# A hybrid decoder layer on one core: the first norm's root one step earlier, and four first loads issued from ACT's queue

## The chip, the cores and the metric

The kernel runs on one core of one Trainium2 chip. The core has a matrix engine (PE, TensorE), a vector engine (DVE), a scalar engine (ACT), GpSimd (POOL) and a sync engine (SP), each with its own in-order queue of instructions, and 16 DMA engines that all queues share. DMA transfers are issued by an instruction on SP, ACT or POOL; most of the weights are issued on SP. The metric is the device time of one execution, in microseconds (us). Before the change it was 1701.68 us, the median of 3 runs (1701.42 to 1701.92).

## The reference

One decoder layer is run on 256 prompt rows and on 8 groups of 8 sample rows, together 320 rows of width 2048. All is float32. Cut to what matters:

```python
def rms_norm(x, g):
    xf = x.astype(jnp.float32)
    y = xf * lax.rsqrt(jnp.mean(xf * xf, axis=-1, keepdims=True) + EPS)
    return (y * g.astype(jnp.float32)).astype(x.dtype)

def decoder_layer(x, ...):
    xn = rms_norm(x, g_mix)
    z = xn @ w_in            # parts B, C, h, q, k, v, gate_conv, gate_attn
    u = c_gate * h_conv
    conv_out, conv_state = short_conv(u, conv_prev, w_conv)
    y_conv = (b_gate * conv_out) @ w_conv_out
    attn = ...               # banded window of 128, 16 query heads, 4 kv heads, sinks
    y_attn = attn @ w_attn_out
    merged = sigmoid(gate_c) * y_conv + sigmoid(gate_a) * y_attn
    h = x + merged @ w_o
    hn = rms_norm(h, g_ffn)
    h = h + (silu(hn @ w_gate) * (hn @ w_up)) @ w_down
    return h, conv_state, k_state, v_state
```

The output is a last RMSNorm of h, with the updated key, value and convolution states. What the change touches is the first line, `rms_norm(x, g_mix)`, and the product with the k and v columns of `w_in` that follows it.

## The kernel before

**Layout.** Rows are tokens in the reference; the kernel keeps activations transposed, with 128 of the 2048 features on the partitions and the 320 tokens along the free axis. A block is such a piece of 128 features; there are 16, numbered 0 to 15.

**Two halves for each operand.** Every product is made of three float32r products: each operand is split into a high part (an ACT copy that rounds, `whi` or `xh_t`) and a low part (a DVE subtraction, `wlo` or `xl_t`), and PE accumulates hi x hi, lo x hi and hi x lo. Weights pass through a raw tile `wraw` (4 buffers), filled by a DMA on SP; `split_to` (L92 to L94) makes `whi` on ACT (L93) and `wlo` on DVE (L94), 3 buffers each. A transfer into a raw buffer waits until the split of the tile that was there is done.

**The start.** `x_load(i)` (L223) fetches columns of x: x is cut into five column blocks of 2, 2, 4, 4 and 4 feature blocks (`XB`), and each is three transfers, two of 128 prompt rows and one of 64 sample rows. In block 0 the second prompt transfer is on ACT's queue; all others are on SP's. `g_mix` is loaded on ACT's queue into `vrow` (L231). Nine products on a constant tile (`wm`, L235) come first on PE; then `g_mix` is turned by a PE transpose (`pv`, L237) and copied by DVE (L238).

**The norm.** The gain `g_mix` is applied to x while it is transposed: `x_prep(kc)` (L242) makes three PE transposes of block kc into `pt`, an ACT copy with the scale g_mix to `xh_t` (L247), the DVE remainder `xl_t` (L248), and a DVE copy of the plain x to `hT` (L253). The root of the mean square, one number for each token, is applied only after the product. The squares are summed on ACT (`squares`, L323), 512 columns at a time. `rstd_of` (L175) then scales the sum (L178), and `inv_root` takes Sqrt on ACT (L185, with a load of its function table), a reciprocal on DVE (L186) and one Newton step on DVE (L187, L188, L190). The result `r3` has a token on each partition; three diagonal matrices `dg` (L367, DVE) and three products with ones (`prb`, L368, PE) spread it over all partitions, and DVE copies it to `rb` (L376).

**The first product.** `kv_product` (L268) multiplies x by the 512 k and v columns, with four accumulators, in nine weight tiles of 1, 1 and then seven times 2 feature blocks. `x_prep(kc + 2)` is issued ahead of the last accumulator of block kc, so that x is prepared while PE multiplies. In the last tile (blocks 14 and 15) the order goes by accumulators, and the fourth accumulator's products are placed behind prb. After the product DVE multiplies the accumulators by `rb` (`kT` L378, `vT` L380), which frees them; the next product, q, takes the same accumulators and waits for that.

**The side work.** `start_rest` (L327) is a generator that holds the small work of the start in steps. `tick` runs it to its next `yield`, once behind each weight tile but the last, and once within the last tile, ahead of accumulator 2 of block 14. Step by step, it issues small loads, squares of columns 0 to 511, nothing, squares of columns 512 to 1023, of 1024 to 1535, of 1536 to 2047 with the sum `s3` (L350) and the copy of `st_sb` (L356), nothing, and in the ninth step, within the last tile, the root and prb. A scheduler orders the instructions of each engine from this program order, from dependencies and from hints given by `after(...)`, so a step that moves in the program need not move by as much on every engine.

**What follows.** Behind the first product comes q (four pairs of columns, `load_q`), beside it the k and v rows are written out, and two transfers of 960 KB from DRAM to DRAM (`cache_shift`, L427) shift the caches. They stand on SP's queue behind the last weight transfers of q's first pair and ahead of those of the second. Then come C, H, B, the gates, the two output products, w_o, and the feed-forward products, all bound to the same two-half scheme.

Of the kernel before, what the change touches and what calls it, by code (L numbers as in the profile page):

```python
# [26 lines left out]
P = 128  # L27
# [13 lines left out]
def hybrid_layer(ctx: ExitStack, tc: tile.TileContext, a: dict, o: list):  # L41
    nc = tc.nc
# [19 lines left out]
    def ps_aux(name):  # L62
        return aux.tile([P, 512], F32, tag="aux", name=name)
# [3 lines left out]
    def u(s):  # L67
        uid[0] += 1
        return f"{s}_{uid[0]}"
# [10 lines left out]
    def tmp(tag, name):  # L80
        return wk.tile([P, UL], F32, tag=tag, name=u(name))
# [80 lines left out]
    g_mix = vecs[:, 0:16]  # L162
# [12 lines left out]
    def rstd_of(ss, shape, name, pool, out=None):  # L175

        v = pool.tile(shape, F32, tag=f"rs_v{shape[1]}", name=u(name))
        nc.vector.tensor_scalar(v, ss, 1.0 / D, EPS, op0=ALU.mult, op1=ALU.add)  # L178
        return inv_root(v, shape, name, pool, out)

    def inv_root(v, shape, name, pool, out=None):

        s = pool.tile(shape, F32, tag=f"rs_s{shape[1]}", name=u(name))
        r = pool.tile(shape, F32, tag=f"rs_r{shape[1]}", name=u(name))
        last["root"] = nc.scalar.activation(s, v, AF.Sqrt)  # L185
        nc.vector.reciprocal(r, s)  # L186
        nc.vector.scalar_tensor_tensor(s, r, -0.5, r, op0=ALU.mult, op1=ALU.mult)  # L187
        nc.vector.tensor_mul(s, s, v)  # L188
        out = r if out is None else out
        last["inv"] = nc.vector.scalar_tensor_tensor(out, s, 1.5, r, op0=ALU.add, op1=ALU.mult)  # L190
        return out
# [25 lines left out]
    st = sp.enter_context(tc.tile_pool(name="st", bufs=1))  # L217
    vrow = st.tile([56, P], F32, name="vrow")
# [4 lines left out]
    def x_load(i):  # L223
        cs = slice(sum(XB[:i]) * P, sum(XB[:i + 1]) * P)
        for t, (t0, tn) in enumerate(TOK):
            src = a["x_prompt"][0, t0:t0 + tn, :] if t < 2 else a["x_sample"].flatten_outer_dims()
            eng = nc.scalar if i == 0 and t == 1 else nc.sync
            eng.dma_start(xs[t][:tn, cs], src[:, cs])

    x_load(0)  # L230
    nc.scalar.dma_start(vrow[0:16, :], a["g_mix"][0].rearrange("(k p) -> k p", p=P))  # L231

    wm = ps_aux("wm")
    for _ in range(9):
# [33 lines left out]
    def kv_product(tiles, x_after):  # L268

        ps = [ps_acc(u("kv")) for _ in range(4)]  # L270
        x_prep(0)
        x_prep(1)
        k0 = 0
        for i, n in enumerate(tiles):
            hi, lo = load_kv(k0, n)
            for b in x_after.get(i, ()):
                x_load(b)
            order = [(k, c) for k in range(n) for c in range(4)]
            if k0 + n == KC:
                order.sort(key=lambda kc: kc[1])  # L280
            for k, c in order:
                kc = k0 + k
                if k0 + n == KC and (k, c) == (0, 2):
                    tick()
                if c == 3 and kc + 2 < KC:
                    x_prep(kc + 2)
                for m, (w, x) in enumerate(((hi, xh), (hi, xl), (lo, xh))):
                    with after(*((mark["prb"],) if k0 + n == KC and c == 3 else ())):
                        last["mm"] = nc.tensor.matmul(
                            ps[c][:, :T], w[:, k, c * P:(c + 1) * P], x(kc),  # L290
                            start=(kc == 0 and m == 0), stop=(kc == KC - 1 and m == 2),
                        )
            k0 += n
            if k0 < KC:
                tick()
        return ps
# [7 lines left out]
    def small_loads():  # L304

        behind = nc.gpsimd.tensor_copy(gate, xh_t[:, 3, 0:1].bitcast(F32))
        with after(behind):
            nc.gpsimd.dma_start(rel, a["rel_bias"])
            nc.gpsimd.dma_start(oh, a["c_onehot"])
            nc.gpsimd.dma_start(sink_bc, sk[0].partition_broadcast(P))  # L310
            nc.gpsimd.dma_start(sink_s, bass.AP(sk.tensor, sk.offset, [[1, NH], [0, TS], [1, 1]]))
            nc.gpsimd.dma_start(vrow[16:32, :], a["g_ffn"][0].rearrange("(k p) -> k p", p=P))
            nc.gpsimd.dma_start(vrow[32:56, :], a["w_conv"][0].rearrange("j (c p) -> (j c) p", p=P))
            nc.gpsimd.dma_start(srow, a["state_conv"][0].rearrange("b j d -> (b j) d"))
            nc.gpsimd.dma_start(blk, a["c_block"])
# [4 lines left out]
    def squares(h):  # L320
        for t, (t0, tn) in enumerate(TOK):
            junk = wk.tile([P, 512], F32, tag="junk", name=u("junk"), bufs=1)
            nc.scalar.activation(  # L323
                junk[:tn, :], xs[t][:tn, h * 512:(h + 1) * 512], AF.Square, accum_out=ss[:tn, t, h:h + 1]
            )

    def start_rest():  # L327
        yield
        small_loads()
        yield  # L330
        squares(0)
        yield
        yield
        squares(1)
        pw = ps_aux("pw")
        nc.tensor.transpose(pw[:, 0:56], vrow, ident[:56, :56])
        nc.vector.tensor_copy(vecs[:, 16:56], pw[:, 16:56])
        yield
        squares(2)
        nc.vector.tensor_scalar(nsink, sink_bc, -1.0, None, op0=ALU.mult)  # L340
        pe_ = ps_aux("pe_")
        nc.tensor.matmul(pe_[:NH, :WIN], rel, oh, start=True, stop=True)
        e_sb = st.tile([NH, EL], F32, name="e_sb")
        nc.vector.memset(e_sb, NEG)
        nc.vector.tensor_copy(e_sb[:, WIN - 1:2 * WIN - 1], pe_[:NH, :WIN])
        nc.gpsimd.dma_start(e_scr, e_sb)
        yield
        squares(3)
        s3 = st.tile([P, 3], F32, name="s3")
        nc.vector.tensor_reduce(s3, ss, axis=AX.X, op=ALU.add)  # L350
        pst = ps_aux("pst")
        for c in range(8):
            nc.tensor.transpose(
                pst[:, c * 16:(c + 1) * 16], srow[:, c * P:(c + 1) * P], ident[:16, :16]
            )
        nc.vector.tensor_copy(st_sb.rearrange("p c s -> p (c s)"), pst[:, 0:128])  # L356
        nc.gpsimd.dma_start(
            bias_s, bass.AP(e_scr.tensor, e_scr.offset + WIN - TS, [[EL, NH], [1, TS], [1, WIN + TS]])
        )
        yield  # L360
        yield
        r3 = rstd_of(s3, [P, 3], "r3", st)
        prb = ps_aux("prb")
        mark["rb"] = prb
        for t, (t0, tn) in enumerate(TOK):
            dg = st.tile([P, P], F32, name=f"dg{t}")
            nc.vector.tensor_scalar(dg[:tn, :tn], ident[:tn, :tn], r3[:tn, t:t + 1], None, op0=ALU.mult)  # L367
            mark["prb"] = nc.tensor.matmul(  # L368
                prb[:, t0:t0 + tn], ones[:tn, :], dg[:tn, :tn], start=True, stop=True
            )  # L370

    side_work[0] = start_rest()
    ps_kv = kv_product([1, 1] + [2] * 7, {0: (1,), 2: (2,), 3: (3,), 4: (4,)})
    for _ in side_work[0]:
# [360 lines left out]
    for cp in range(4):  # L735
        c_sb = []
        ps = in_pair(O_C + cp * CW, "C")
        for c in range(2):
            t = tmp("ta", "csb")
# [30 lines left out]
        for c in range(2):  # L770
            ch = cp * 2 + c
            cv, cs = conv[c]
            t = tmp("td", "bc")
# [46 lines left out]
    for mp in range(8):  # L820
        c0 = mp * CW
        sg = {}
        for nm, off, tag in (("gc", O_GC, "ta"), ("ga", O_GA, "tb")):
            ps = in_pair(off + c0, nm)
            for c in range(2):
                t = tmp(tag, nm)[:, :T]
# [12 lines left out]
        for c in range(2):  # L839
            t = sg["ga", c]  # L840
# [11 lines left out]
    for mp in range(8):  # L852
# [5 lines left out]
        for c in range(2):  # L858
            k = mp * 2 + c
# [8 lines left out]
            else:  # L868
                t = tmp("tc", "sq")[:, :T]
# [8 lines left out]
    for half in range(2):  # L878
# [5 lines left out]
        for fpair in range(nf // 2):  # L884
# [10 lines left out]
            for c in range(2):  # L895
                t, t2 = tmp("ta", "gs")[:, :T], tmp("tb", "sg")[:, :T]
# [51 lines left out]
        for mp in range(8 if half == 0 else 7):  # L948
# [5 lines left out]
            for c in range(2):  # L954
                k = mp * 2 + c
                nc.vector.tensor_add(hT[:, k, :], hT[:, k, :], ps[c][:, :T])
            if half == 1:
                pc = [to_rows(mp * 2 + c) for c in range(2)]
                for c in range(2):
                    k = mp * 2 + c  # L960
# [125 lines left out]
```

## Time and profile before

| What | Value |
|---|---|
| Median of 3 runs | 1701.68 us (1701.42 to 1701.92) |
| The profiled execution | 1700.47 us, span 1698.7 us, TensorE clock 0.998 |
| PE busy | 1686.0 us (99%) |
| DVE, ACT, POOL busy | 868.8, 644.6, 81.3 us |
| DMA over the span | 258.22 MB, mean 152 GB/s |
| First product (`kv`) on PE | from 7.29 us to about 47 us |
| One 128x128 by 128x320 product, start to start | 0.147 us |

The page gives the busy time of each engine, the chain of work that ended last, and the groups of instructions. A line of the list of waits reads: the engine that waited, the tile it was to write and its line, then what ended the wait; total us, times, longest us. A line of the timeline reads: start us, duration us, engine, line, operation, out<-in, shapes, count (a merged line's duration runs from the first start to the last end), and in brackets the idle time of that engine just before and what ended it. Matmul records overlap, since they are pipelined: each lasts 0.31 us and the next starts 0.147 us after it.

### The profile page before, as it was taken

The numbers are of one execution on the slowest core, as the hardware profiler recorded it, in microseconds if no ns is written. First come the engines' busy times: TensorE is split into PE (matmuls) and PEld (weight loads), VectorE is DVE, ScalarE is ACT, GpSimd is POOL, SyncE is SP. The second block draws the span as 40 slices with busy tenths as digits, with TensorE's granted clock in tenths as the row PEclk, the third lists the DMA queues.
The fourth block names the chain that finished last, engine by engine and source line by source line (L and its number), as shares of the span: only waits on it lengthen the run. The fifth ranks groups of instructions, "written<-read, shape, count | busy, mean of one in ns | idle before, by whom it ended". The sixth has DMA issues, their size and how long they took to land.

```text
span 1698.7 us, 27819 instructions
## 1 busy us (share of the span) xinstructions
PE 1686.0 (99%) x11640; PEld 1673.2 (98%) x11640; DVE 868.8 (51%) x1259; ACT 644.6 (38%) x940; POOL 81.3 (5%) x127
## 2 busy tenths in 40 slices
PE   9999999999999999999999999999999999999997
PEld 8999999999999999999999999999999999999997
DVE  6667654444444445555454545433335555554444
ACT  6445443333333333334333333322233333333343
POOL 1001221000000001220000000000000000000000
PEclk9999999999999999999999999999999999999999
DMA  7654544554454444444444544444444444445443
GB/s 219 208 154 138 160 151 137 151 149 149 149 149 149 149 150 150 150 150 148 151 150 151 151 152 151 149 149 149 149 150 149 149 150 150 151 152 168 150 143 106
DMA packets 256654, 258.22 MB, mean 152 GB/s; under 512 B 9090, under 2 KB 251486, under 8 KB 256368
## 3 DMA queue, kind: packets, MB, share of 16 engines
q1 hardware_dynamic: 254144, 250.12, 47.6%
q0 software_dynamic: 2128, 5.92, 1.1%
q8 instruction: 91, 1.49, 0.4%
q10 hardware_dynamic: 256, 0.40, 0.1%
q14 instruction: 35, 0.29, 0.0%
HBM read 253.29 MB, written 5.08 MB: 152 GB/s over the span
## 4 chain that ended last, share of the span: by engine, by line
PE 97%; DVE 0%; issue 0%; ACT 0%; DVEq 0%; ACTq 0%
PE fu L134 18%; PE fg L134 18%; PE dn L134 17%; PE wo L134 7%; PE gc L134 7%; PE ga L134 7%; PE C L134 3%; PE B L134 3%; PE H L134 3%; PE ya L134 3%; PE yc L134 3%; PE q L134 3%; PE dr L1005 1%; PE fa L935 0%; PE po L518 0%; PE pp L505 0%
## 5 line engine op out<-in xcount | busy, mean ns | idle before, releaser
L94 DVE TENSOR_TENSOR wlo<-wraw,whi 128x1024 fp32r<-128x1024 f32 (+1 forms) x479 | 571.5, 1196 | 692.6 <-ACT whi L93 690.0
L93 ACT ACTIVATE whi<-wraw 128x1024 fp32r<-128x1024 f32 (+1 forms) x479 | 491.2, 1030 | 841.9 <-PE dn L134 192.1
L134 PE MATMUL dn<-a_t,whi 128*128 128x320 f32 x1328 | 293.4, 309 | 0.0
L134 PEld LDWEIGHTS dn<-a_t,whi 128*128 128x128 f32 x1328 | 221.5, 188 | 0.0
L134 PE MATMUL fu<-hh_t,whi 128*128 128x320 f32 x704 | 217.2, 309 | 0.0
L134 PE MATMUL fg<-hh_t,wlo 128*128 128x320 f32 x704 | 217.1, 308 | 0.0
L134 PE MATMUL fg<-hh_t,whi 128*128 128x320 f32 x704 | 217.1, 308 | 0.0
L134 PE MATMUL fg<-hl_t,whi 128*128 128x320 f32 x704 | 217.1, 308 | 0.0
L134 PE MATMUL fu<-hl_t,whi 128*128 128x320 f32 x704 | 217.0, 308 | 0.0
L134 PE MATMUL fu<-hh_t,wlo 128*128 128x320 f32 x704 | 217.0, 308 | 0.0
L134 PE MATMUL dn<-a_t,wlo 128*128 128x320 f32 x664 | 204.8, 308 | 0.0
L134 PEld LDWEIGHTS fu<-hl_t,whi 128*128 128x128 f32 x704 | 132.1, 188 | 0.1
L134 PEld LDWEIGHTS fu<-hh_t,whi 128*128 128x128 f32 x704 | 132.1, 188 | 0.1
L134 PEld LDWEIGHTS fg<-hl_t,whi 128*128 128x128 f32 x704 | 132.1, 188 | 0.0
L134 PEld LDWEIGHTS fg<-hh_t,wlo 128*128 128x128 f32 x704 | 132.1, 188 | 0.0
L134 PEld LDWEIGHTS fg<-hh_t,whi 128*128 128x128 f32 x704 | 132.1, 188 | 0.0
L134 PEld LDWEIGHTS fu<-hh_t,wlo 128*128 128x128 f32 x704 | 132.1, 188 | 0.0
L134 PEld LDWEIGHTS dn<-a_t,wlo 128*128 128x128 f32 x664 | 124.6, 188 | 0.0
L134 PE MATMUL gc<-xh_t,whi 128*128 128x320 f32 x256 | 79.5, 311 | 0.0
L134 PE MATMUL ga<-xh_t,whi 128*128 128x320 f32 x256 | 79.4, 310 | 0.0
L134 PE MATMUL ga<-xl_t,whi 128*128 128x320 f32 x256 | 79.4, 310 | 0.0
L134 PE MATMUL ga<-xh_t,wlo 128*128 128x320 f32 x256 | 79.4, 310 | 0.0
(298 smaller groups left out, 2851.3 us busy)
## 6 DMA issues: line engine op xcount, KB each, us to landing
wraw<-in_w_in_dram SPq DMA_DIRECT2D x119, 512.0 KB, 3.7
wraw<-in_w_gate_dram SPq DMA_DIRECT2D x88, 512.0 KB, 3.6
wraw<-in_w_up_dram SPq DMA_DIRECT2D x88, 512.0 KB, 3.6
wraw<-in_w_down_dram SPq DMA_DIRECT2D x88, 512.0 KB, 3.5
wraw<-in_w_o_dram SPq DMA_DIRECT2D x32, 512.0 KB, 3.5
wraw<-in_w_in_dram SPq DMA_DIRECT2D x34, 256.0 KB, 4.3
wraw<-in_w_conv_out_dram SPq DMA_DIRECT2D x16, 512.0 KB, 3.5
wraw<-in_w_attn_out_dram SPq DMA_DIRECT2D x32, 256.0 KB, 3.9
```

Source lines behind the costliest of these rows:

```text
L93: last["hi"] = nc.scalar.activation(hi, src, AF.Copy)
L94: last["lo"] = nc.vector.tensor_sub(lo, src, hi.bitcast(F32))
L134: last["mm"] = nc.tensor.matmul(ps[c][:, :T], w[:, k, c * P:(c + 1) * P], x(kc), start=(kc == 0 and i == 0), stop=(kc == nk - 1 and i == 2),)
L1005: nc.tensor.matmul(ps[:, :CW], x, w, start=(k == 0 and m == 0), stop=(k == nf - 1 and m == len(ms) - 1))
```

## The change

Two edits. First, which queue issues some of the first loads: `x_load` sends three transfers instead of one to ACT's queue (the second prompt rows of block 0 as before, and the sample rows of blocks 0 and 1), and the load of `g_mix`, already on ACT's queue, is issued ahead of `x_load(0)` instead of behind it. So g_mix is the first transfer on ACT's queue, then the prompt rows, then the two of the sample rows, and SP's queue has two transfers fewer. Second, in `start_rest` the call of `rstd_of` moves ahead of a `yield`: the root is issued with the eighth step, behind the tile of blocks 12 and 13, and dg and prb stay in the ninth, within the last tile.

```diff
@@ x_load
         for t, (t0, tn) in enumerate(TOK):
             src = a["x_prompt"][0, t0:t0 + tn, :] if t < 2 else a["x_sample"].flatten_outer_dims()
-            eng = nc.scalar if i == 0 and t == 1 else nc.sync
+            eng = nc.scalar if (i, t) in ((0, 1), (0, 2), (1, 2)) else nc.sync
             eng.dma_start(xs[t][:tn, cs], src[:, cs])
 
+    nc.scalar.dma_start(vrow[0:16, :], a["g_mix"][0].rearrange("(k p) -> k p", p=P))
     x_load(0)
-    nc.scalar.dma_start(vrow[0:16, :], a["g_mix"][0].rearrange("(k p) -> k p", p=P))
@@ start_rest
         yield
-        yield
         r3 = rstd_of(s3, [P, 3], "r3", st)
+        yield
         prb = ps_aux("prb")
         mark["rb"] = prb
```

More of the change, by code (lines that the diff above doesn't have):

```diff
@@ L360, in start_rest @@
         yield
+        r3 = rstd_of(s3, [P, 3], "r3", st)
         yield
-        r3 = rstd_of(s3, [P, 3], "r3", st)
         prb = ps_aux("prb")
```

## The prediction

> **What bounds the kernel now.** I read the page first, then who waits on PE, then the order in time around each PE stall.
>
> ```profile
> PE 1686.0 (99%) x11640; PEld 1673.2 (98%) x11640; DVE 868.8 (51%) x1259; ACT 644.6 (38%) x940; POOL 81.3 (5%) x127
> PE 97%; DVE 0%; issue 0%; ACT 0%; DVEq 0%; ACTq 0%
> ```
>
> PE is busy 99% of the span and is 97% of the chain that ended last. Engines other than PE cost nothing by themselves; a change pays what it takes out of, or puts into, PE's idle time. PE's whole list of waits is four lines:
>
> ```profile
> PE prb L368 <- DVE dg L367: 1.8, 1, 1.8
> PE wm L235 <- DVE busy L160: 1.6, 1, 1.6
> PE kv L289 <- ACT whi L93: 0.3, 1, 0.3
> PE kv L289 <- DVE wlo L94: 0.2, 1, 0.2
> ```
>
> The first is what the moved root feeds; the third and fourth lie in the start, where the moved loads are; the second is the launch. In time, the end of the first product:
>
> ```profile
> 36.32 0.28 DVE L356 COPY st_sb<-pst 128x128 f32<-128x128 f32 x1
> 37.78 0.53 ACT L247 ACTIVATE xh_t<-pt,vecs 128x320 fp32r<-128x320 f32 x1 [2.36 <-PE pt L246]
> 38.34 0.55 DVE L248 SCALAR_TENSOR_TENSOR xl_t<-pt,vecs,xh_t 128x320 fp32r<-128x320 f32 x1 [1.74 <-ACT xh_t L247]
> 40.20 0.52 ACT L247 ACTIVATE xh_t<-pt,vecs 128x320 fp32r<-128x320 f32 x1
> 40.43 0.16 DVE L178 TENSOR_SCALAR r<-s 128x3 f32<-128x3 f32 x1
> 40.73 1.28 ACT L185 ACT_TABLE_LOAD   x1
> 42.02 0.21 ACT L185 ACTIVATE r<-r 128x3 f32<-128x3 f32 x1
> 42.87 0.31 PE L289 MATMUL kv<-xh_t,wlo 128*128 128x320 f32 x1
> 44.28 0.15 DVE L190 SCALAR_TENSOR_TENSOR r<-r,r 128x3 f32<-128x3 f32 x1
> 44.55 0.64 DVE L367 TENSOR_SCALAR dg<-ident,r 128x128 f32<-128x128 f32 x3
> 44.98 1.04 PE L368 MATMUL prb<-dg,ones 128*128 128x128 f32 x6 [1.80 <-DVE dg L367]
> 46.06 0.49 DVE L376 COPY rb<-prb 128x320 f32<-128x320 f32 x1 [0.87 <-PE prb L368]
> 46.59 0.89 DVE L378 TENSOR_TENSOR kT<-kv,rb 128x320 f32<-128x320 f32 x2
> 47.13 0.41 PE L134 MATMUL q<-xh_t,whi 128*128 128x320 f32 x1
> ```
>
> The reader is to see that PE ran out of work: matmuls follow each other every 0.147 us, so after the one at 42.87 the next could go at 43.02; prb went at 44.95 to 44.98, because its operand dg stands at the end of a row: L178, table load, Sqrt, four small DVE operations, dg. And from 35.43 (when ACT's previous block ended) to 37.78 ACT was idle for 2.36 us, with 1.74 us on DVE beside it. In the start:
>
> ```profile
> 9.28 0.63 ACT L93 ACTIVATE whi<-wraw 128x512 fp32r<-128x512 f32 x1 [1.41 <-DMA wraw<-in_w_in_dram]
> 9.97 0.42 PE L289 MATMUL kv<-xh_t,whi 128*128 128x320 f32 x1 [0.32 <-ACT whi L93]
> ```
>
> PE lost 0.48 us (9.49 to 9.97) to the second weight tile, and 0.36 more at 13.25 (next possible 12.89) to the third tile's wlo.
>
> **The root.** Nothing is added or removed: the same table load (1.28), Sqrt (0.21), five small DVE operations (0.15 to 0.17 each), three dg (0.64) and three prb products. In the instruction order of the changed kernel L178 to L190 stand on DVE behind the st_sb copy and ahead of the xl_t of block 14; the table load and Sqrt stand on ACT ahead of the xh_t of block 14; dg0 and dg1 behind the last weight tile's wlo; and prb behind 13 instead of 18 matmuls of the last tile, so that 11 matmuls lie behind it.
>
> ACT: the table load can start at 35.43 and ends at 36.71. L178 follows the st_sb copy (ends 36.60): 36.76. Sqrt 36.8 to 37.0. The next on ACT, xh_t of block 14, waits for PE until 37.78: it is covered by 0.8 us. DVE: four operations of 0.17 + 3 x 0.15 = 0.62, and some 0.1 between dependent ones: r is ready near 37.95. Behind it waits xl_t of block 14, which could not start before 38.34: covered by 0.4 us. If the cover were gone, xl_t, hT, the last wlo (39.29 to 40.51, for which PE already stalled 0.15 at 40.57) and the matmuls behind them slip one for one.
>
> PE then: the last tile's 13 matmuls go at 40.12, 40.27, 40.57 and on to 42.14. dg0 and dg1 take 40.51 to 40.95, block 15's xl_t 41.0 to 41.55 (its matmul is at 41.70: close, 0.1 us), hT to 42.0, dg2 to 42.2. prb starts at 42.29 without waiting and takes 1.0 (44.95 to 45.95 before): 43.29. The 11 matmuls end at 43.29 + 11 x 0.147 = 44.90.
>
> What is late next: q's first matmul needs the accumulator that kT reads. On DVE stand dg2, two wlo of q's first tile (0.66 + 0.69, to 43.5), the rb copy (0.49, to 43.95), one more wlo (0.67, to 44.6) and then kT (0.45 for the first): 45.1. So PE waits about 0.2 there (before 0.20, at 47.13) and q starts near 45.15: 47.13 - 45.15 = 1.98 us earlier. The ends: 2.2 if kT is no longer late, 1.2 if the table load does not fit the gap (below).
>
> Does the 1.98 reach the end? Only what is fixed in time could take it back: DMA. SP issues the two cache copies (960 KB each) at 41.68 and 42.56, and the weights issued behind them at 43.36 and 43.83 land 13.4 and 13.8 us later, at 57.6. Their split on ACT took 57.70 to 58.85, and wlo would then end at 59.65. SP's issue at 43.36 waits for the second wlo of q's first tile, 43.02 before and 43.5 now, so add 0.15. PE needs that wlo at 62.7 before, and at 60.7 now: 0.9 us of room is left. That cover has shrunk from 3, but it is there. Later splits wait for PE, no more for DMA (the last wait on wraw is that of 57.70). The rest of the instruction order is unchanged. I take 0 here, with 0.5 loss as the far end.
>
> **The loads.** x block 0's and 1's sample rows leave SP (issues of 0.59 and 0.48 us) for ACT, and g_mix goes ahead of x's second row group there. ACT then issues g_mix at 0.74, prompt rows at 1.2, samples at 1.65 and about 2.1, and its first table load (1.67 to 2.95) moves to about 2.7 to 4.0; it is needed at 5.57. SP: the first weights are issued at 1.2, not 1.82; the second tile's issue at 4.08 waited for the prompt rows sent on ACT at 0.74 (3.3 us to landing) and waits now for g_mix, so it may go as early as 2.7.
>
> What that is worth: PE's first real work (pv, 5.55) follows its nine warm-up products (1.60 + 9 x 0.427 = 5.45), not a load; g_mix, asked for at 1.19, was down by 5.02, when SP issued what waits on it. So g_mix gains nothing. First weights: whi at 5.57 has room until xh_t at 6.71. Second and third weight tile: DMA moved 234 to 281 GB/s from 2 to 8 us against 335 at most at 12 to 14 us; the bytes ahead of these tiles are the same 0.9 MB. Issuing sooner fills dips only. Ends: 0.84 gained (both stalls gone), 0.3 lost (samples third in ACT's queue). I take 0.1 gained, nearest to the DMA rows, which show a full engine.
>
> **Sum.** 1.98 + 0.1 = 2.1 us. The profiled execution took 1700.47 (span 1698.70 and 1.77 around it) and becomes 1698.4, span 1696.6. The median of the runs is 1.21 above it, so 1701.68 becomes **1699.6**. What a measurement of this kernel tells from no change is 0.2%, 3.4 us; this lies inside.
>
> **Rivals.**
> 1. *The table load does not fit.* [...] Against it: before, ACT's xh_t ended at 40.72 and the load began at 40.73 and Sqrt at 42.02, nothing between. Chance 0.12. [...]
> 2. *The start gains too*: the second and third weight tile come 0.5 to 0.8 earlier. Both stalls go: 1698.9. For it: wraw's issue at 4.08 is freed. Against it: DMA is full. Chance 0.10.
> 3. *The gain is swallowed* at the weights behind the cache copies, or at kT: 0 to 0.9 left, 1701.0. Chance 0.08.
> 4. *Slower: the sample rows come late.* PE's third transpose, near 6.1, needs them; they land 3.3 after 1.65, at 4.95, but with the 7.5 us that a later sample load took at 9.15. PE would start 3.0 us later: 2.0 gained, 3.0 lost, 1702.7. It decides from a landing at 8.2 on; over 0.2% from 11.7. Chance 0.06.
> 5. *As forecast*, 1699.0 to 1700.1: 0.64.
>
> 1698.4 to 1700.9 holds the forecast and rivals 1 and 2 with the runs' own spread (1701.42 to 1701.92), 0.86, less a little for what was not thought of. Cases beyond 3.4 us: faster needs the 2.2 and both start stalls and more, 0.05; slower 0.05; within 0.90.
>
> **What would show it.** Right: PE's wait at prb gone from the waits; table load between 35.4 and 37; Sqrt before 37.1; q's first matmul at 45.1 to 45.3 with a short wait for kT; whi near 57.8 still the last to wait for DMA. Wrong: a wait of kv for xl_t or wlo of over 0.5 us near 40 to 42; a first kv matmul much after 7.29; a PE wait near 60.7.

## The result and the profile after

In a common series the changed kernel took 1697.08 us (median of 11 executions, 1696.58 to 1698.14) and the kernel before 1701.45 (11 executions, 1700.30 to 1701.92): ratio 0.9975, 95% interval 0.9966 to 0.9984. It is 4.4 us faster. The forecast was 1699.6 with a range from 1698.4; the gain is twice the 2.1 us that the sum had, and the time lies below the range.

The profiled execution of the changed kernel took 1697.49 us (span 1695.7), against 1700.47 (span 1698.7) before: 2.98 us between these two, not 4.4. Much of this section and the next is about the difference.

First the busy times from the page, then the whole list of PE's waits:

```profile
PE 1684.7 (99%) x11640; PEld 1672.7 (99%) x11640; DVE 868.9 (51%) x1259; ACT 644.5 (38%) x940; POOL 81.5 (5%) x127
...
PE 98%; issue 1%; DMA 0%; DVE 0%; ACT 0%; POOL 0%; DVEq 0%; ACTq 0%; POOLq 0%
```

```profile
PE wm L235 <- DVE busy L160: 1.6, 1, 1.6
PE q L134 <- DVE wlo L94: 0.4, 1, 0.4
PE kv L289 <- ACT xh_t L247: 0.3, 1, 0.3
```

The 1.8 us wait of prb for dg is gone, and so are the waits for the second and third weight tile. New are 0.4 us of q for a wlo and, in the start, 0.3 us of kv for xh_t. The timeline at the end of the first product:

```profile
33.84 0.53 ACT L247 ACTIVATE xh_t<-pt,vecs 128x320 fp32r<-128x320 f32 x1 [0.62 <-PE pt L246]
34.39 1.28 ACT L185 ACT_TABLE_LOAD   x1
...
35.69 0.20 ACT L185 ACTIVATE r<-r 128x3 f32<-128x3 f32 x1
...
36.56 0.16 DVE L190 SCALAR_TENSOR_TENSOR r<-r,r 128x3 f32<-128x3 f32 x1
36.73 0.53 ACT L247 ACTIVATE xh_t<-pt,vecs 128x320 fp32r<-128x320 f32 x1 [0.84 <-PE pt L246]
...
40.63 0.24 DVE L367 TENSOR_SCALAR dg<-ident,r 64x64 f32<-64x64 f32 x1
...
41.23 0.97 PE L368 MATMUL prb<-dg,ones 128*128 128x128 f32 x6
42.24 0.49 DVE L376 COPY rb<-prb 128x320 f32<-128x320 f32 x1 [0.17 <-PE prb L368]
...
43.25 0.88 DVE L378 TENSOR_TENSOR kT<-kv,rb 128x320 f32<-128x320 f32 x2
...
43.85 0.35 PE L134 MATMUL q<-xh_t,whi 128*128 128x320 f32 x1
```

The root now lies in ACT's gap: the table load starts 0.02 us after the xh_t copy, Sqrt 0.02 us after the load, r is complete at 36.72, and block 14's xh_t still waits 0.84 us for PE. dg stands ready at 40.87, prb carries no wait, and q starts at 43.85 with no wait for kT, whose first half ran at 43.25.

How the gain builds up shows when the same matmul (by its number in PE's order) is looked up in both traces. At the 100th, the changed kernel is 1.05 us ahead; the 250th, among the last ahead of prb, is as far ahead; at q's first (the 268th) it is 3.28 ahead, from q's third on 3.35; q's wait for wlo, at 63.50, gives back 0.40; from there to the end the distance is 2.95 without change. So in these two executions the start gave 1.05, the moved root 2.2 at q's first matmul and 2.3 from its third on, and 0.4 was lost.

### The profile page after: what moved, and what is told of

Its sections match the earlier page's. It is cut to its first block, busy times and chain, and to the rows that moved or that the text cites. A ratio compares the mean times of both kernels' runs of the same rounds, so it can differ in the third digit from the quotient of the medians.

```text
span 1695.7 us, 27814 instructions
## 1 busy us (share of the span) xinstructions
PE 1684.7 (99%) x11640; PEld 1672.7 (99%) x11640; DVE 868.9 (51%) x1259; ACT 644.5 (38%) x940; POOL 81.5 (5%) x127
## 4 chain that ended last, share of the span: by engine, by line
PE 98%; issue 1%; DMA 0%; DVE 0%; ACT 0%; POOL 0%; DVEq 0%; ACTq 0%; POOLq 0%
PE fg L134 18%; PE fu L134 18%; PE dn L134 17%; PE wo L134 7%; PE gc L134 7%; PE ga L134 7%; PE C L134 3%; PE B L134 3%; PE H L134 3%; PE ya L134 3%; PE yc L134 3%; PE q L134 2%; PE kv L289 1%; PE dr L1005 1%; DMA out_dram<-kn 0%
```

## The experiments

Each kernel was timed beside the kernel before on the same chip, 9 to 11 executions each; the kernel before stood at 1701.04 in the first series (33 executions), 1701.08 in the second (31) and 1701.15 in the third (21). Ratios are to that, with a 95% interval.

### One part alone

The root's move alone:

```diff
         yield
-        yield
         r3 = rstd_of(s3, [P, 3], "r3", st)
+        yield
```

> The root's move alone, the loads as before. Theory A (the two edits add up, the loads are worth 1.05 us in the start): 2.0 to 2.3 us faster than before, PE's wait at prb gone, second and third weight tile split at 9.3 and 10.9 us as before. Theory B (the loads are worth no more than the 0.1 us that was predicted, and all the rest belongs to the root): 3 to 4.3 us faster. Theory C (the runs of before lose more in the start than its one profiled execution shows): 2.0 to 2.3 us faster, and as wide a gap between its profiled run and its median as before had.

It took 1697.77 us (1697.43 to 1698.54), ratio 0.9985 (0.9976 to 0.9993): 3.27 less than before. Its profiled execution (1697.43, span 1695.7) shows the gap closed, and nothing lost behind it:

```profile
PE wm L235 <- DVE busy L160: 1.6, 1, 1.6
PE kv L289 <- ACT whi L93: 0.4, 1, 0.4
PE kv L289 <- ACT xh_t L247: 0.3, 1, 0.3
```

From the 250th matmul to q's third passed 3.10 us, in the changed kernel's trace the same, and 5.39 before: 2.3 us. The trace explains 2.3 of the 3.27; one microsecond is missing.

The loads alone:

```diff
-            eng = nc.scalar if i == 0 and t == 1 else nc.sync
+            eng = nc.scalar if (i, t) in ((0, 1), (0, 2), (1, 2)) else nc.sync
...
+    nc.scalar.dma_start(vrow[0:16, :], a["g_mix"][0].rearrange("(k p) -> k p", p=P))
     x_load(0)
-    nc.scalar.dma_start(vrow[0:16, :], a["g_mix"][0].rearrange("(k p) -> k p", p=P))
```

> The loads alone, the root as before. Theory A: 1.0 to 1.2 us faster in the runs as in the trace, the second weight tile split at 8.5 us and the third at 9.8, prb still waiting 1.8 us for dg. Theory B: 0 to 0.2 us. Theory C: 2.0 to 2.4 us faster in the runs, 1.0 in the trace against the trace of before that was shown.

1700.37 us (1699.03 to 1700.92), ratio 0.9996 (0.9987 to 1.0005). By medians 0.67 less, but the interval holds 1. In its trace prb still waits 1.8 us for dg.

Then each half of that edit alone, g_mix first (the second hunk), and the sample rows on ACT's queue (the first hunk):

> Only g_mix moved ahead of the prompt rows on ACT's queue; the sample rows stay on SP. The issue of the second weight tile then waits for g_mix and not for the prompt rows, but SP still has the sample rows' two issues in front. If that wait sets the weights' time: issue at 3.9 (SP free) and not 4.08, so a gain of 0.2 us at most. If the competing sample rows on SP set it: no gain.

> Only the sample rows of blocks 0 and 1 moved to ACT's queue; g_mix behind the first of them. SP has two issues less, but the second weight tile's issue waits again for the prompt rows sent at 0.74, which land near 4.0. If that wait sets the weights' time, there is no gain in the start, and possibly 0.2 us of loss at PE's first transposes. If SP's shorter queue does it: second tile's split 0.6 to 0.8 us earlier, 0.5 to 0.8 us faster.

g_mix first: 1701.05 us, ratio 1.0002 (0.9993 to 1.0011): nothing; SP issued the second weight tile at 3.91, as in the kernel before when it was run again. The sample rows: 1700.56 (1699.14 to 1701.01), ratio 0.9994 (0.9985 to 1.0003). This interval holds 1 too; by the medians and by the traces below, what the loads do is done by the sample rows. How, the stretches of the start show (us; PE, PEld, DVE, ACT, POOL busy; granted clock; DMA share; GB/s), before:

```profile
4.00:6.00 2.00, 2.00 (x6) 0.71 (x5) 0.12 (x1) 0.43 (x1) 0.00 (x0) 1.00 0.76 241
6.00:8.00 2.00, 2.00 (x11) 1.62 (x11) 1.47 (x4) 1.26 (x3) 0.00 (x0) 1.00 0.81 281
```

and after:

```profile
4.00:6.00 2.00, 2.00 (x7) 0.68 (x5) 0.13 (x2) 0.79 (x2) 0.00 (x0) 1.00 1.01 325
6.00:8.00 2.00, 1.70 (x12) 1.29 (x11) 1.54 (x5) 0.95 (x2) 0.00 (x0) 1.00 1.00 322
```

From 4 to 8 us the DMA share was 0.76 to 0.81 before and 1.00 to 1.01 after. For 4 to 6 us all traces agree: 0.70 to 0.84 (198 to 259 GB/s) in the seven with all sample rows on SP, 0.96 to 1.12 (290 to 325 GB/s) in the five with some on ACT's queue; for 6 to 8 us the two sets overlap. SP issues the second weight tile at 3.49 instead of 4.08 (3.90 to 3.92 in the other traces with all sample rows on SP, 3.48 to 3.62 in those with some of them on ACT's queue), and the splits of the second and third tile on ACT, before:

```profile
9.28 0.63 ACT L93 ACTIVATE whi<-wraw 128x512 fp32r<-128x512 f32 x1 [1.41 <-DMA wraw<-in_w_in_dram]
10.88 1.06 ACT L93 ACTIVATE whi<-wraw 128x1024 fp32r<-128x1024 f32 x1 [0.55 <-DMA wraw<-in_w_in_dram]
```

and after:

```profile
8.50 0.63 ACT L93 ACTIVATE whi<-wraw 128x512 fp32r<-128x512 f32 x1 [1.00 <-DMA wraw<-in_w_in_dram]
9.82 1.06 ACT L93 ACTIVATE whi<-wraw 128x1024 fp32r<-128x1024 f32 x1
```

came 0.78 and 1.06 us earlier. Not all of that is the edit: the 100th matmul stood 0 (the first profile itself), 0.18, 0.21, 0.25, 0.59, 0.72 and 0.75 us ahead of the first profile's in the seven traces with all sample rows on SP, and in the five with some on ACT's queue 0.82, 0.88, 1.05, 1.10 and 1.46. The means are 0.39 and 1.06: some 0.7 us for the loads, in single executions that vary by as much, though the two sets do not overlap.

### Does the kernel before repeat

> The kernel before, unchanged, to see how far its profiled execution varies. Theory A: no difference, within 0.3 us, and a trace like the first, span near 1698.7. Theory C: no difference in the runs, but a trace with a span near 1699.7 and up to 1 us more waiting for DMA in the first 14 us.

The same kernel again: 1701.25 us (1699.99 to 1702.30), ratio 1.0002 (0.9993 to 1.0011). Its profile is the most telling of all, since it took 1701.48, one microsecond more than the first profile of the same program. Its span, 1699.7, is the one that theory C named, but not by theory C's cause: at the 100th matmul it was 0.18 us ahead of the first profile, so its start as a whole cost no more. The stretches around prb (columns as above; the seventh figure is the granted clock):

```profile
42.00:44.00 2.00, 1.00 (x7) 0.73 (x5) 1.93 (x6) 1.08 (x3) 0.00 (x0) 1.00 1.47 431
44.00:46.00 2.00, 1.22 (x7) 1.01 (x7) 0.88 (x5) 0.00 (x0) 0.00 (x0) 0.89 0.16 42
46.00:48.00 2.00, 2.00 (x8) 2.00 (x9) 1.88 (x5) 0.32 (x1) 0.00 (x0) 0.50 0.99 365
48.00:50.00 2.00, 2.00 (x12) 2.00 (x11) 2.00 (x5) 0.84 (x2) 0.00 (x0) 0.76 0.51 215
```

and in the first profile:

```profile
46.00:48.00 2.00, 1.97 (x13) 1.71 (x13) 1.91 (x5) 0.96 (x2) 0.00 (x0) 1.00 0.91 335
48.00:50.00 2.00, 2.00 (x15) 2.00 (x15) 2.00 (x5) 0.20 (x1) 0.00 (x0) 1.00 0.32 131
```

From 45.55 to 48.96 TensorE ran at half its clock: 8 matmuls in the 2 us where the other execution has 13. PE is "busy" all the while, so no list of waits shows it. Between the 250th and the 290th matmul this execution lost 1.2 us on the first one, since matmuls follow each other every 0.267 us in that stretch. The gap ahead of prb thus costs twice: the 1.8 us in which PE waits, and in some executions 3.41 us of half clock behind it. The same stretch stands in the profiles of g_mix alone (44.98 to 48.40) and of the sample rows alone (45.12 to 48.53), and in none of the four with the moved root. Of five traces with the gap, three have it.

The times say how often. The second series' 31 executions of the kernel before fall in two groups with nothing between: 15 from 1699.84 to 1700.78 (median 1700.21) and 16 from 1701.08 to 1702.19 (median 1701.40), 1.19 us apart. The sample rows alone do the same: five from 1699.14 to 1699.45, six from 1700.56 to 1701.01; both loads together: five from 1699.03 to 1699.60, six from 1700.37 to 1700.92. Each of the five profiled executions of kernels with the gap stands in the group that its trace asks for: 1700.47 and 1699.60 without a half-clock stretch in the lower, 1701.48, 1701.05 and 1700.81 with one in the upper. The mean granted clock points the same way: it is 0.997 in nine of the upper sixteen executions and in none of the lower fifteen. In the first and the third series the kernel before shows no such break: between 1699.6 and 1701.7 no two neighbouring times are over 0.3 us apart, so that the two groups rest on the second series, on the sample rows alone and on both loads together.

### Filling the gap without closing it

To hold the gap and take away only its effect on the clock, PE is given useless work in it: products on the constant tile, written into prb's buffer and overwritten by prb.

```diff
         mark["rb"] = prb
+        for _ in range(8):
+            nc.tensor.matmul(prb, busy[:, :P], busy, start=True, stop=True)
```

> The kernel before with eight idle products (128x128 by 128x512, results overwritten) put on PE ahead of prb, so that PE is not idle while prb's operand is made; no other step moves, but one matmul of the first product falls behind prb (0.15 us). Clock theory (a hole of 1.9 us in one clock window sometimes halves TensorE's granted clock for the next 3.4 us, about 1.0 us lost in such an execution): prb still starts near 45, no stretch at half clock between launch and end, 0.3 to 0.9 us faster than before in the median and a narrower spread. Rival (the extra microsecond of the root's move comes from DVE or DMA): no faster than before, 0.1 to 0.2 us slower, stretches at half clock still seen.

1700.21 us (1699.66 to 1701.78), ratio 0.9995 (0.9987 to 1.0004). The median is where the lower group of the kernel before is (1700.21), 0.87 under its median, and the trace has no half-clock stretch; one execution of the eleven, 1701.78, lies where the upper group does. By the interval alone this could be no change, so the gap was made longer and the pair repeated: ten small DVE operations on r3 (multiplied by 1.0) between the root and dg, and the same with 16 products in the gap.

```diff
         r3 = rstd_of(s3, [P, 3], "r3", st)
+        for _ in range(10):
+            nc.vector.tensor_scalar(r3, r3, 1.0, 0.0, op0=ALU.mult, op1=ALU.add)
...
         mark["rb"] = prb
+        for _ in range(16):
+            nc.tensor.matmul(prb, busy[:, :P], busy, start=True, stop=True)
```

> Kernel before with ten more small DVE operations on the root r3 (each multiplies it by 1.0) between the root and dg, so that PE's gap ahead of prb grows from some 2 to some 3.7 us, longer than one 3.41 us stretch of the clock. Clock theory: a gap of 2 us halves the clock only where it falls well in a stretch, so the kernel before has two groups of times, some 1.2 us apart (1699.8 to 1700.8 and 1701.1 to 1702.2); a gap of 3.7 us leaves no such choice, each execution has a stretch of 3.413 us at half clock, and the times make one group: 1700.2 + 1.8 + 1.2 = 1703.2, and about 1.2 above the filled twin. The trace shows a granted clock of 0.5 within 45 to 53 us. Rival, the two groups have another cause (the start): two groups again, 1702.0 and 1703.2, and the same times as the filled twin.

> The same ten DVE operations, with sixteen 128x128x512 bf16 products on the constant tile written into prb's buffer ahead of the real prb, so that PE stays busy in the longer gap; prb overwrites what they write. Clock theory: no stretch at half clock, one group of times at 1700.2 + 1.8 = 1702.0, up to 0.3 more if the sixteen products outlast the gap, some 1.2 under the unfilled twin. Rival (another cause of the two groups): no difference from the unfilled twin, two groups.

The longer gap took 1704.25 us (1703.38 to 1706.15), ratio 1.0020 (1.0011 to 1.0029); filled, 1702.19 (1701.37 to 1703.23), ratio 1.0007 (0.9998 to 1.0016). Not one execution of the first is as quick as the slowest of the second. The mean granted clock, which each execution reports, is 0.996 or 0.997 in all eleven of the first, 0.998 or 0.999 in all eleven of the second. The profiled ones took 1703.44 and 1702.20. In the first, the timeline has

```profile
46.76 1.22 PE L370 MATMUL prb<-dg,ones 128*128 128x128 f32 x6 [3.82 <-DVE dg L369]
47.91 0.63 PE L289 MATMUL kv<-xh_t,whi 128*128 128x320 f32 x1
48.34 0.47 PE L289 MATMUL kv<-xl_t,whi 128*128 128x320 f32 x1
48.60 0.47 PE L289 MATMUL kv<-xh_t,wlo 128*128 128x320 f32 x1
```

and in the filled one

```profile
46.70 1.07 PE L372 MATMUL prb<-dg,ones 128*128 128x128 f32 x6 [0.56 <-DVE dg L371]
47.70 0.42 PE L289 MATMUL kv<-xl_t,whi 128*128 128x320 f32 x1
47.96 0.31 PE L289 MATMUL kv<-xh_t,wlo 128*128 128x320 f32 x1
```

prb starts at the same time in both, 46.76 and 46.70, so the data are no later; only behind it do they part, with matmuls of 0.47 us against 0.31 and 0.27 us from start to start against 0.147. In the first the granted clock was 0.50 from 48 to 50 us, in the second 1.00 in every stretch from 42 to 52 us: that the gap halved the clock, and that filling it prevented that, is shown for these two. The size was expected at 1.2: the two profiled executions are 1.24 apart, the medians 2.06. Nor do the times of the longer gap make one group, as was expected: they spread over 2.8 us. The six with a mean clock of 0.996 reach from 1703.83 to 1706.15, but 1706.02 has 0.997, so the mean clock does not settle it. None of these slower executions was traced, and what more they lost stays open.

### The changed kernel again, and a variant

> The changed kernel again, beside the others on one chip. Clock theory: 3.5 to 4.5 us faster than before, no stretch at half clock between launch and end. If the edits only add what their traces show apart (2.2 for the root and 0.7 for the loads): 2.9 us.

> The changed kernel with the sample rows of block 0 back on SP's queue (those of block 1 stay on ACT's, g_mix stays first, the root stays moved). The second weight tile is issued when g_mix has landed, near 3.5, or when SP is free, near 3.5: as in the changed kernel. The sample rows of block 0 land about 0.5 us earlier, so PE's third transpose waits no more for them. 0 to 0.3 us faster than the changed kernel, so 3.6 to 4.6 us faster than before.

The changed kernel again: 1697.20 us (1696.72 to 1697.35), ratio 0.9977 (0.9967 to 0.9987). In its trace q's matmuls, from the third on, stand 3.75 us ahead of the first profile of before, and q's wait for wlo gives back about 0.57. The variant with block 0's sample rows left on SP and only block 1's on ACT,

```diff
-            eng = nc.scalar if (i, t) in ((0, 1), (0, 2), (1, 2)) else nc.sync
+            eng = nc.scalar if (i, t) in ((0, 1), (1, 2)) else nc.sync
```

took 1697.11 (1696.84 to 1698.67), ratio 0.9979 (0.9971 to 0.9988), with its trace 3.40 ahead and nothing given back. By time the two can't be told apart; no version beat the changed kernel.

## Why the prediction was wrong

**What bounds the kernel: right, but read from one kind of execution.** PE's idle time was the right place to look, and the list of waits was complete for the execution that was profiled. But that execution had no half-clock stretch and the median of 1701.68, by its time, belonged to the others: of the eleven executions in the common series only one, 1700.30, is as quick as the profiled one. The prediction wrote "The median of the runs is 1.21 above it", and carried these 1.21 us over to the changed kernel as if they were a fixed offset. They were a cost of the gap: the two groups of before are 1.19 apart, and with the gap closed the changed kernel's median, 1697.08, lies 0.41 under its profiled execution, not 1.21 above it. This is the step that failed first. A term was missing from the sum: the gap's effect on the clock, about 1.2 us in the executions in which the median lies. (The executions of the common series were not traced; that the median one had the stretch is read from its time.)

**The root: the mechanism right, 1.98 measured as 2.2 to 2.3.** Table load in ACT's gap, r ready before block 14's xl_t, the wlo of the last tile not delayed, prb without a wait: each came as written, with r at 36.72 (37.95 was forecast; the start's 1.05 us taken off, 36.90). One size was off. The wait of q for kT, put at 0.2, did not come: DVE was done with the two wlo ahead of rb at 42.07 (the forecast's 43.5, less 1.05, is 42.45), so rb came right behind prb (42.24), and kT's first half was done ahead of q's first matmul. The end named for that case, 2.2, is what the four traces with the moved root show there: 2.22 to 2.23 at q's first matmul, 2.29 to 2.30 from its third on.

**The table load that does not fit (rival 1): excluded.** Nothing stood between the load's end at 35.67 and Sqrt at 35.69, and 0.02 us stood ahead of the load. The load took 1.28 us, as before, and Sqrt 0.20. No run shows the 1.2 us that the prediction had as the low end of the root's gain for this case, nor the part of its range that was for it: the four traces with the moved root show 2.22 to 2.23 at q's first matmul.

**The loads: 0.1 was too small; some 0.6 to 0.9.** The argument was "the bytes ahead of these tiles are the same" and, in rival 2, "DMA is full". The bytes were the same, but the rows that were read, 234 to 281 GB/s, were not those of full engines: from 4 to 6 us the changed kernel moves 325 GB/s, and the DMA share of 0.76 in the row of before said that there was room. The second tile landed at 8.34 to 9.30 us in the seven traces with all sample rows on SP (mean 8.86) and at 7.03 to 8.48 in the five others (mean 7.78), so its landing moved with its issue. By the groups of the second series: the sample rows alone have medians of 1699.34 and 1700.81, before has 1700.21 and 1701.40, so 0.6 to 0.9; by the changed kernel against the root alone, 1697.77 less 1697.08 or 1697.20, 0.6 to 0.7; by the mean of the traces 0.7. The intervals of both direct comparisons take in no gain at all, so the size is known only roughly. Rival 2 had the mechanism and gave it 0.10.

**What is late next: right in kind.** q's wait for wlo behind the cache copies, held for possible with "0.5 loss as the far end", came with 0.40 and about 0.57 in the changed kernel's two traces, at 63.50 and 63.27, one tile later than the forecast looked, and not at all in the root alone and the variant. The variant is as far ahead (3.40 against 3.35 and 3.75), so being early is not the whole of it. What differs is the fourth weight transfer behind the cache copies: SP issued it at 51.07 and 51.77 in the two with the wait and it landed at 58.95 and 58.72, against 48.73 and 46.55, and 57.22 and 57.05, in the two without. Why it was issued so much later stays open. In the changed kernel's trace, what followed was:

```profile
59.06 1.15 ACT L93 ACTIVATE whi<-wraw 128x512 fp32r<-128x512 f32 x2 [1.32 <-DMA wraw<-in_w_in_dram]
...
60.55 0.42 DVE L721 TENSOR_TENSOR at_h<-qt,at_h 64x256 fp32r<-64x256 f32 x1 [0.39 <-ACT at_h L720]
...
63.50 0.41 PE L134 MATMUL q<-xh_t,wlo 128*128 128x320 f32 x1 [0.45 <-DVE wlo L94]
```

The late split held up small attention work on ACT and DVE (L720, L721), and the wlo that PE waited for, at 62.75, stood behind that work.

**The rival on the other side** (sample rows late) showed only as 0.2 us of a transpose waiting for its sample rows in the trace of the loads alone. The three reorderings of loads without the moved root came out even with before or below it.

**The sum.** From the median of before in the common series: 1701.45 less 1.2 (the half-clock stretch that the median execution had) less 2.3 (the gap) less 0.6 to 0.9 (the loads) plus up to 0.6 (q's wlo) gives 1697.05 to 1697.95, against 1697.08 measured. That is the low end: with q's wait as both traces show it, 0.40 to 0.57, the sum is 1697.45 to 1697.92, and the 0.4 to 0.8 that is left stays open. With the terms of the prediction and the missing one, 1.98 + 0.1 + 1.2 = 3.3 us, the time would have been 1698.4 from 1701.68, the lower end of the range; most of the rest is the loads.

## What to carry to other kernels

Where the median of a kernel lies a microsecond away from its profiled execution, look for something that happens in some executions only, and list all times before calling the difference an offset. A gap on TensorE is to be priced with what may follow it: here its length, 1.8 us, and in three traces of five a stretch of half clock of 3.4 us behind it, which cost another 1.2 us and which no list of waits shows, since PE counts as busy (2.00 of 2 us at a clock of 0.50, 46 to 48 us in the repeated kernel before). And GB/s alone do not say that the DMA engines are full: at 241 GB/s with a share of 0.76 an earlier issue was an earlier landing. A share near 1 is no ceiling either, since a row above has 1.47 with 431 GB/s.

## What the runs showed of the hardware

TensorE's clock was halved by a gap that is shorter than the stretch over which it is lowered: 1.8 us of waiting (2.1 from the last matmul's start to prb's, where 0.147 is usual) was enough in three traces of five. Each of the three lowered stretches lasted 3.41 to 3.42 us (45.55 to 48.96, 44.98 to 48.40, 45.12 to 48.53), and they start on a grid: in the repeated kernel before, the trace's first record of the full clock is at 4.59 and the fall at 45.55, 40.96 later, which is 12 times 3.413; in the two others it is 37.547, 11 times. In the first trace of before and in that of the changed kernel, which have no such stretch, the record of the full clock starts at 7.18 and 5.78 and lasts 1686.184 us in both, 494 times 3.4133; from there to the end of the span, the last 5.3 and 3.8 us, the clock is 0.50. The grid lies differently in each execution (that first record was seen from 4.59 to 7.57 us), so where the gap falls in it differed too. In the first profile of before the grid cell that holds most of the gap, 41.31 to 44.73, had 1.71 us of matmuls (each counted with 0.147) and no stretch followed; in the repeated one the cell from 42.14 to 45.55 had 1.47, and the clock was halved behind it. The other traces agree: 1.47 in g_mix alone and in the sample rows alone and 0.72 in the longer gap, each followed by a stretch; 1.88 in the loads alone and at least 2.8 in all those with the gap closed or filled, with none. An estimate from these: the limit lies between 1.47 and 1.71 us of a cell of 3.41. A gap of 1.95 us then halves the clock where it lies wholly within one cell, or nearly so, which by the same numbers is 0.43 to 0.57 of the positions. The second series has 16 of 31 in its upper group; the common series has 10 of 11 above 1701, more than this accounts for, and that stays open.
